# Down blocks of seven products: four sums after the next block's first splits, transfers in another order, two accumulators filled one after the other

## The chip, the cores and the metric

One core of a Trainium2 chip runs the kernel. The metric is the device time of one execution in microseconds; of several runs the median is given. The weights and inputs lie in HBM, and the result is written there.

## The reference, cut to what matters

Two layers work on 512 tokens of width 1024. Each layer mixes (layer 0 by gated projections, layer 1 by attention, both with attention to a memory) and then has a feed-forward part, which is where the change lies:

```python
f = rmsnorm(h, ln_ffn_pre[layer])
f = (jax.nn.silu(f @ w_ffn_gate[layer]) * (f @ w_ffn_up[layer])) @ w_ffn_down[layer]
h = h + rmsnorm(f, ln_ffn_post[layer])
```

The hidden width is 2816, that is 22 blocks of 128. Everything is float32.

## The kernel before, in words

**Exact products by parts.** A float32 operand is split into a high and a low half (`split`, L238 and L239): ScalarE casts the high half (`whi`), VectorE subtracts to get the low one (`wlo`). A product is then three matmuls (`mm3`, L189 to L193): high by high, and two of high by low. TensorE can only begin a product when ScalarE and VectorE have split its weights.

**Seven products for eight.** Two blocks of a matrix product are done by seven products in place of eight, with sums of the operands before and sums of the results after (a scheme of the Strassen kind). There are two sorts of such blocks.

- A gate block and an up block (`Seven`, L1018) work on two blocks of hidden units each. Two loads of 512 KB give four quarters a11, a12, a21, a22. `sums` (L1037) adds them in place (L1041, L1043, L1045, L1046) and splits the first two; `run(n)` does product n. `sevens` (L1088) runs gate, then up, each with the products in the order 1, 7, 2, 6, 4, 3, 5. The results lie in PSUM: tile `a` (called `p` in the code) for products 1, 6 and 5, tile `e` for 7 and 4, tile `x` for 2 and 3. After product 1, ScalarE copies `a` to `s1` (L1059), and product 6 goes on adding to the same `a`. A product is 12 matmuls of 256 columns.
- A down block (`DownSeven`, L1182, and `down_sevens`, L1228) takes four hidden blocks, as two units a and b, to the 1024 outputs of all four token blocks. It has six accumulators of 128x512 in PSUM: two in `chain` (tiles `yc`), two in `shared` (`ys`) and two in `lows` (`yl`), one of each pair for the first and one for the second token block of a half. A product of one unit into one accumulator is three matmuls of 512 columns.

**Where results gather.** `ys[tb][dh]` (tiles `y` in the profile) are eight tiles of 128x512 in SBUF, for four token blocks tb and two output halves dh. A result is added to them in one of two ways. `put` (L1230) has ScalarE copy the accumulator to a tile `yo` (L1232), and GpSimd issue a transfer of 256 KB that adds it to `y` (L1234). Or VectorE adds the accumulator directly (L1262, L1265, L1268). An addition to a tile waits for the one before it on the same tile.

**The order of a down block.** Products 1 (chain), 7 (shared), 2 (lows) of unit a; then of unit b product 1, `put` of the chain to (x, 0), product 7, `put` of shared to (x, 1) and to (x + 2, 1); product 6 of both into the chain, whose value so far ScalarE copies into `shared` (L1256); product 2 of unit b; product 5 of both (chain), `put` to (x + 2, 1), and VectorE adds lows to (x, 0) (L1262); product 4 of both into shared, added to (x, 1) by L1265; product 3 of both into the chain, added to (x + 2, 0) by L1268. Here x is 0 or 1. `both` does a product of unit a into the two accumulators, then that of unit b.

**Groups.** `feed_forward` (L1113) does, per layer, five groups of four hidden blocks: two pairs of gate and up blocks, then a down block. The fifth group has no down block; its result goes through `tail_of`. So there are four down blocks in each layer, eight in all, and each is followed by a gate block. While these run, VectorE makes the splits, the sums of quarters and the sums of results, all in one queue in order; ScalarE casts and copies; SyncE issues the loads of weights (four buffers `raw` of 512 KB, taken in turn); GpSimd issues the adding transfers. Eight buffers each serve `whi` and `wlo`, taken in turn.

**What sets the order.** A framework orders the instructions of each engine from the order of the code and its own guess of times; `tc.high_priority` and `behind` push some forward or back. In the program before, VectorE's queue at a down block's end has the two sums L1265 ahead of the next gate block's second split, and the two sums L1268 ahead of L1046 and of the split of product 7.

Of the kernel before, what the change touches and what calls it, by code (L numbers as in the profile page):

```python
# [11 lines left out]
ALU = mybir.AluOpType  # L12
# [3 lines left out]
P = 128  # L16
# [24 lines left out]
def hybrid(ctx: ExitStack, tc: tile.TileContext, i: dict, out: bass.AP):  # L41
# [17 lines left out]
    def act(s, dt=F32R, shape=(P, T)):  # L59
        return ap.tile(list(shape), dt, tag="a", name=name(s))  # L60

    def plain(s, shape=(P, T), dt=F32):
        return yp.tile(list(shape), dt, tag="y", name=name(s))

    def prob(s, shape=(P, T)):
        return tp.tile(list(shape), F32, tag="p", name=name(s), bufs=6)
# [4 lines left out]
    def small(s, n=4, dt=F32):  # L71
        return sp.tile([P, n], dt, tag=f"s{n}", name=name(s))

    def ps(tag, shape=(P, T), s="ps"):
        return pp.tile(list(shape), F32, tag=tag, name=name(s), bufs=2 if tag == "tr" else 3)

    V, A, PE, G = nc.vector, nc.scalar, nc.tensor, nc.gpsimd
# [102 lines left out]
    def down_weights(layer, k, dh, aside=False):  # L180
        return moving_pair(i["w_down"][layer, 4 * dh : 4 * dh + 4, :, k : k + 2, :]
                           .rearrange("m p k c -> p m (k c)"), aside)
# [6 lines left out]
    def mm3(o, w, x, start, stop, more=False):  # L189

        PE.matmul(o, w[0], x[0], start=start, stop=False, skip_group_check=more)  # L191
        PE.matmul(o, w[0], x[1], start=False, stop=False, skip_group_check=more)  # L192
        return PE.matmul(o, w[1], x[0], start=False, stop=stop, skip_group_check=more)  # L193
# [44 lines left out]
    def split(src, hi, lo, eng=None):  # L238
        last_parts[:] = A.copy(hi, src), (eng or V).tensor_sub(lo, src, hi)  # L239
# [6 lines left out]
    @contextmanager  # L246
    def behind(some):

        with ExitStack() as s:
            for ins in some:  # L250
                s.enter_context(tc.issue_after(ins.ins))
            yield
# [832 lines left out]

    ended = [None]

    def sevens(pair, plain_first, opens=False):  # L1088

        if not plain_first:  # L1090
            for make in pair:
                u = make()
                with behind(ended if opens else ()):
                    u.sums()
                opens = False
                for n in (1, 7, 2, 6, 4, 3, 5):
                    u.run(n)
                u.end()
            return
        us = []  # L1100
        for make in pair:
            us.append(make())
            us[-1].sums()
            for n in (1, 2, 3):
                us[-1].run(n)
        for some in ((7, 6), (4, 5)):
            for u in us:
                for n in some:
                    u.run(n)
        for u in us:  # L1110
            u.end()

    def feed_forward(layer, phase, xp, meanwhile=None):  # L1113
# [24 lines left out]
        def up_rows(row, u, fs, done):  # L1138
            if row:
                V.scalar_tensor_tensor(out=u, in0=u, scalar=-1.0, in1=gates[1], op0=ALU.mult, op1=ALU.mult)  # L1140
            else:
                V.tensor_mul(u, u, gates[0])
            if done:
                done(row, u)
            else:
                split(u, *fs[len(fs) - 2 + row])
# [35 lines left out]
        class DownSeven:  # L1182
# [30 lines left out]
                split_aside(src, *(t.rearrange("p (m c) -> p m c", m=4) for t in pair), aside)  # L1213
                return pair

            def product(self, outs, n, start, stop):
                w = self.w[n]
                if n == 2:
                    w = self.parts(w)
                    V.tensor_add(self.a[1], self.a[0], self.a[1])  # L1220
                    self.w[3] = self.a[1]
                elif n != 1:
                    w = self.parts(w)
                for x, o in enumerate(outs):
                    c = slice(x * P, (x + 1) * P)
                    mm3(o, tuple(t[:, c] for t in self.x[n]), w, start, stop, True)

        def down_sevens(us, pairs):  # L1228

            def put(x, *where):  # L1230
                some = prob("yo")
                A.copy(some, x)  # L1232
                for tb, dh in where:
                    G.dma_start(ys[tb][dh], some, accum_op=ALU.add)  # L1234

            def both(outs, n):
                a.product(outs, n, False, False)
                b.product(outs, n, False, True)

            a, b = us  # L1240
            a.sums(pairs[0])
            chain, shared, lows = ([ps(t, s=n) for _ in range(2)] for t, n in (("tr", "yc"), ("lg", "ys"), ("mm", "yl")))
            a.product(chain, 1, True, False)
            a.product(shared, 7, True, False)
            a.product(lows, 2, True, False)
            b.sums(pairs[1])
            b.product(chain, 1, False, True)
            for x in range(2):
                put(chain[x], (x, 0))
            b.product(shared, 7, False, True)  # L1250
            for x in range(2):
                put(shared[x], (x, 1), (x + 2, 1))
            both(chain, 6)
            with tc.high_priority():
                for x in range(2):
                    A.copy(shared[x], chain[x])  # L1256
            b.product(lows, 2, False, True)
            both(chain, 5)
            for x in range(2):
                put(chain[x], (x + 2, 1))  # L1260
            for x in range(2):
                V.tensor_add(ys[x][0], lows[x], ys[x][0])  # L1262
            both(shared, 4)
            for x in range(2):
                V.tensor_add(ys[x][1], shared[x], ys[x][1])  # L1265
            both(chain, 3)
            for x in range(2):
                V.tensor_add(ys[x + 2][0], chain[x], ys[x + 2][0])  # L1268

        fs = [(act("fhi"), act("flo")) for _ in range(2)]  # L1270

# [8 lines left out]
        a, close = boundary(phase, G_MIX_POST + layer, G_FFN_PRE + layer, nnorm, rb, first, evac_first, scaled)  # L1280
        w = [down_weights(layer, 0, dh) for dh in range(2)]
# [3 lines left out]
        ys = [[plain("y") for _ in range(2)] for _ in range(TB)]  # L1285
        for tb in range(TB):
            for dh in range(2):
                o = ps("lg" if dh else "mm", s="y")
                for k in range(2):
                    token_products(o, fs[k], w[dh][k], tb, k == 0, k == 1)  # L1290
                A.copy(ys[tb][dh], o)

        for gi, (k0, k1) in enumerate(groups):
            fs, pairs, downs = [], [], []
            for m in range(k0, k1, 2):
                if meanwhile and m == k1 - 2 and gi == len(groups) - 1:
                    next(meanwhile)
                if gi < len(groups) - 1:
                    pairs.append(Inner(m < k1 - 2))
                    if m > k0:  # L1300
                        downs.append(DownSeven(m, True))
                else:
                    fs += [(act("fhi"), act("flo")) for _ in range(2)]
                sevens((lambda: Seven(xs, lambda n: i["w_gate"][layer, m + n], "mm", gate_rows),
                        lambda: Seven(xs, lambda n: i["w_up"][layer, m + n], "lg",
                                      lambda row, t: up_rows(row, t, fs, pairs and pairs[-1]))), m == 2, m == k0)
            nk = k1 - k0
            if gi == len(groups) - 1:
                if layer:
                    with behind([gates[2]]):  # L1310
                        A.preload_act_table_set("natural_log_exp_and_others")
                if meanwhile:
                    next(meanwhile)

                eps = small("eps")
                V.tensor_mul(eps, nnorm.r4, nnorm.r4)
                V.reciprocal(eps, eps)
                V.tensor_scalar_mul(eps, eps, RMS_EPS)
                return tail_of(fs, lambda kp, dh, aside, k0=k0: down_weights(layer, k0 + 2 * kp, dh, aside), ys, eps,
                               layer == 1)  # L1320
            down_sevens([DownSeven(k0, False)] + downs, pairs)


    def layer_b(phase, fp):
# [194 lines left out]
    with tc.tile_pool(name="ffn0", bufs=4) as xp:  # L1519
        phase = feed_forward(0, phase, xp, memory())  # L1520
    with tc.tile_pool(name="fox", bufs=1) as fp:
        phase = layer_b(phase, fp)
    with tc.tile_pool(name="ffn1", bufs=4) as xp:
        tail, ys = feed_forward(1, phase, xp)
# [97 lines left out]
```

## Time and profile before

| what | value |
|---|---|
| median of 3 runs | 1107.38 us |
| the three runs | 1107.38, 1107.46, 1104.4 us |
| the profiled execution, its own time | 1104.82 us |
| its span, first to last instruction | 1103.1 us |
| mean granted TensorE clock | 0.998 |
| busy: TensorE, VectorE, ScalarE, GpSimd | 98%, 88%, 68%, 9% |
| mean traffic of the DMA queues | 127 GB/s |

The table gives whole-span figures. Matmuls are pipelined, and the profile draws one of 256 columns 0.28 us long where the next starts sooner, so a busy TensorE shows only its longer waits as idle. In the lines shown below, `out<-in` are tiles by the program's names, `x` with a number is a count, and a bracket at the end of a row gives the idle time of the engine just before it and what ended that. PEld is TensorE's loading of weights, DVE is VectorE, ACT ScalarE, POOL GpSimd, SP SyncE; a q behind an engine is its queue.

### The profile page before, as it was taken

Reading aid. Unit: us, or ns where it says so; the run is one execution under the profiler, and the core shown is the slowest. Engines: PE = TensorE matmul, PEld = TensorE weight load, DVE = VectorE, ACT = ScalarE, POOL = GpSimd, SP = SyncE. Lnnn points to the kernel's source line nnn. Section 1 sums busy time; section 2 is a strip of 40 time slices with the busy share of each in tenths; the row PEclk is TensorE's granted clock in tenths of the full one; section 3 lists DMA queues with packets and bytes.
Section 4 is the critical chain, followed back from the end, with each engine's and each line's share of the span. In section 5 each row is a group of like instructions: output and inputs, shape, how many; then the busy total and the mean of one; then the engine's idle time right before and its main releaser. Section 6 shows DMA issues by size and latency. Waiting matters only on the chain.

```text
span 1103.1 us, 19756 instructions
## 1 busy us (share of the span) xinstructions
PE 1082.6 (98%) x7266; PEld 983.3 (89%) x7267; DVE 970.7 (88%) x1942; ACT 754.5 (68%) x1588; POOL 93.8 (9%) x120
## 2 busy tenths in 40 slices
PE   9999999999999999999999999999999999999998
PEld 7998889997979899998988998889997979899996
DVE  7879759998999999997968789868999989999986
ACT  7776578665756757677746788868666756756664
POOL 0000000002020201101000000000002020201100
PEclk9999999999999999999999999999999999999999
DMA  7521331338464664746222654531338464564722
GB/s 269 160 82 51 120 116 39 115 97 191 120 158 125 136 173 97 207 134 193 68 86 59 154 136 120 148 115 40 115 97 191 116 159 129 116 173 106 180 97 77
DMA packets 83992, 139.64 MB, mean 127 GB/s; under 512 B 6772, under 2 KB 49800, under 8 KB 83896
## 3 DMA queue, kind: packets, MB, share of 16 engines
q1 hardware_dynamic: 71480, 116.57, 34.4%
q0 software_dynamic: 11712, 21.50, 11.7%
q8 instruction: 57, 0.93, 0.4%
q10 hardware_dynamic: 704, 0.32, 0.1%
q14 instruction: 39, 0.32, 0.1%
HBM read 105.23 MB, written 2.10 MB: 97 GB/s over the span
## 4 chain that ended last, share of the span: by engine, by line
PE 85%; DVE 5%; DMA 5%; ACT 3%; issue 1%; SPq 1%; POOL 0%; DVEq 0%; ACTq 0%
PE a L193 5%; PE a L192 5%; PE a L191 5%; PE y L191 4%; PE y L193 4%; PE y L192 4%; PE ps L191 4%; PE ps L193 4%; PE ps L192 4%; DMA y<-yo 4%; PE e L193 3%; PE e L192 3%; PE e L191 3%; PE x L193 3%; PE x L192 3%; PE x L191 3%
## 5 line engine op out<-in xcount | busy, mean ns | idle before, releaser
L239 ACT CAST whi<-raw 128x512 fp32r<-128x512 f32 x444 | 260.7, 619 | 117.9 <-DVE raw L1045 58.2
L239 DVE TENSOR_TENSOR wlo<-raw,whi 128x512 fp32r<-128x512 f32 x444 | 290.6, 682 | 21.0 <-ACT whi L239 20.3
L193 PE MATMUL x<-xshi,wlo 128*128 128x256 f32 x320 | 90.4, 282 | 0.2 <-DVE wlo L239 0.2
L192 PE MATMUL x<-xslo,whi 128*128 128x256 f32 x320 | 90.1, 282 | 0.0
L191 PE MATMUL x<-xshi,whi 128*128 128x256 f32 x320 | 90.1, 282 | 0.0
L192 PE MATMUL a<-xslo,whi 128*128 128x256 f32 x320 | 89.9, 281 | 0.0
L191 PE MATMUL a<-xshi,whi 128*128 128x256 f32 x320 | 89.8, 281 | 0.0
L193 PE MATMUL a<-xshi,wlo 128*128 128x256 f32 x320 | 89.7, 281 | 0.0
L1234 POOL DMA_DIRECT2D y<-yo x64 | 55.5, 1143 | 196.9 <-ACT yo L1232 135.0
L191 PE MATMUL ps<-xshi,whi 128*128 128x256 f32 (+1 forms) x224 | 68.4, 306 | 0.0
L192 PE MATMUL ps<-xslo,whi 128*128 128x256 f32 (+1 forms) x224 | 66.7, 298 | 0.0
L193 PE MATMUL ps<-xshi,wlo 128*128 128x256 f32 (+1 forms) x224 | 66.3, 298 | 0.0
L239 ACT CAST whi<-s 128x512 fp32r<-128x512 f32 x56 | 34.7, 620 | 41.0 <-DVE s L1205 25.0
L193 PEld LDWEIGHTS x<-xshi,wlo 128*128 128x128 f32 x320 | 60.6, 189 | 0.4 <-DVE wlo L239 0.4
L191 PEld LDWEIGHTS a<-xshi,whi 128*128 128x128 f32 x320 | 60.2, 188 | 0.4
L192 PEld LDWEIGHTS a<-xslo,whi 128*128 128x128 f32 x320 | 60.2, 188 | 0.4
L192 PEld LDWEIGHTS x<-xslo,whi 128*128 128x128 f32 x320 | 60.5, 189 | 0.0
L191 PEld LDWEIGHTS x<-xshi,whi 128*128 128x128 f32 x320 | 60.5, 189 | 0.0
L193 PEld LDWEIGHTS a<-xshi,wlo 128*128 128x128 f32 x320 | 60.2, 188 | 0.0
L193 PE MATMUL e<-t3hi,wlo 128*128 128x256 f32 x160 | 45.7, 286 | 10.5 <-DVE wlo L239 10.5
L191 PE MATMUL y<-whi,mixedhi 128*128 128x512 f32 x128 | 51.3, 401 | 0.0
L192 PE MATMUL y<-wlo,mixedhi 128*128 128x512 f32 x128 | 50.6, 395 | 0.0
(352 smaller groups left out, 3637.4 us busy)
## 6 DMA issues: line engine op xcount, KB each, us to landing
raw<-in_w_gate SPq DMA_DIRECT2D x44, 512.0 KB, 3.7
raw<-in_w_up SPq DMA_DIRECT2D x44, 512.0 KB, 5.3
y<-yo POOLq DMA_DIRECT2D x64, 256.0 KB, 5.8
raw<-in_w_down SPq DMA_DIRECT2D x28, 512.0 KB, 4.6
raw<-in_w_out SPq DMA_DIRECT2D x16, 512.0 KB, 4.0
wd<-in_w_down SPq DMA_DIRECT2D x32, 256.0 KB, 8.8
flo<-s POOLq DMA_DIRECT2D x16, 256.0 KB, 5.1
raw<-in_w_b_q SPq DMA_DIRECT2D x8, 512.0 KB, 4.4
```

Source lines behind the costliest of these rows:

```text
L191: PE.matmul(o, w[0], x[0], start=start, stop=False, skip_group_check=more)
L192: PE.matmul(o, w[0], x[1], start=False, stop=False, skip_group_check=more)
L193: return PE.matmul(o, w[1], x[0], start=False, stop=stop, skip_group_check=more)
L239: last_parts[:] = A.copy(hi, src), (eng or V).tensor_sub(lo, src, hi)
L1234: G.dma_start(ys[tb][dh], some, accum_op=ALU.add)
```

## The change

Three edits, all to the down blocks.

1. **Four sums put off.** The last four additions of VectorE, L1265 and L1268, are no longer done at the end of `down_sevens`. It returns them as a function `rest`, with those of the chain now first, and `sevens` calls it in the next group's first gate block, after `run(2)`.
2. **Transfers in another order.** After product 7, the transfers of both accumulators to (x, 1) are issued first, then both to (x + 2, 1). Before, the two transfers of one accumulator stood together. On GpSimd's queue the eight transfers of a block went to (0,0), (1,0), (0,1), (2,1), (1,1), (3,1), (2,1), (3,1); now they go to (0,0), (1,0), (0,1), (1,1), (2,1), (3,1), (2,1), (3,1).
3. **Token block first.** `both` makes the splits of both units first, and then does units a and b into the first accumulator, and units a and b into the second.

```diff
-    def sevens(pair, plain_first, opens=False):
+    def sevens(pair, plain_first, opens=False, rest=None):
...
                 for n in (1, 7, 2, 6, 4, 3, 5):
                     u.run(n)
+                    if rest and n == 2:
+                        rest()
+                        rest = None
                 u.end()
...
+            def product(self, outs, n, start, stop):
+                w = self.weights(n)
                 for x, o in enumerate(outs):
-                    c = slice(x * P, (x + 1) * P)
-                    mm3(o, tuple(t[:, c] for t in self.x[n]), w, start, stop, True)
+                    self.one(o, x, n, w, start, stop)
+
+            def one(self, o, x, n, w, start, stop):
+                c = slice(x * P, (x + 1) * P)
+                mm3(o, tuple(t[:, c] for t in self.x[n]), w, start, stop, True)
...
             def both(outs, n):
-                a.product(outs, n, False, False)
-                b.product(outs, n, False, True)
+                ws = [u.weights(n) for u in us]
+                for x, o in enumerate(outs):
+                    for u, w in zip(us, ws):
+                        u.one(o, x, n, w, False, u is b)
...
             b.product(shared, 7, False, True)
+            both_sums = [put(shared[x], (x, 1)) for x in range(2)]
             for x in range(2):
-                put(shared[x], (x, 1), (x + 2, 1))
+                G.dma_start(ys[x + 2][1], both_sums[x], accum_op=ALU.add)
...
             both(shared, 4)
-            for x in range(2):
-                V.tensor_add(ys[x][1], shared[x], ys[x][1])
             both(chain, 3)
-            for x in range(2):
-                V.tensor_add(ys[x + 2][0], chain[x], ys[x + 2][0])
+
+            def rest():
+                for x in range(2):
+                    V.tensor_add(ys[x + 2][0], chain[x], ys[x + 2][0])
+                for x in range(2):
+                    V.tensor_add(ys[x][1], shared[x], ys[x][1])
+
+            return rest
...
-            down_sevens([DownSeven(k0, False)] + downs, pairs)
+            rest = down_sevens([DownSeven(k0, False)] + downs, pairs)
```

`weights(n)` is the part of the old `product` that splits the weights of product n; `put` now takes one destination and returns its tile `yo`.

In these rows the lines of the changed kernel are its own: its L1281 and L1283 are L1268 and L1265 of the kernel before. VectorE at the end of the first down block, before (`raw_3323` and `raw_3325` are the next gate block's weights, `s_7` its sum for product 7, `ys` and `yc` the accumulators):

```order
L1043 TENSOR_TENSOR raw_3325<-raw_3325 128x512
L1265 TENSOR_TENSOR y_2472<-ys_3149,y_2472 128x512
L1265 TENSOR_TENSOR y_2474<-ys_3150,y_2474 128x512
L239 TENSOR_TENSOR wlo_3340<-raw_3323,whi_3339 128x512
L1045 TENSOR_TENSOR raw_3323<-raw_3325,raw_3323 128x512
L1268 TENSOR_TENSOR y_2475<-yc_3147,y_2475 128x512
L1268 TENSOR_TENSOR y_2477<-yc_3148,y_2477 128x512
L1046 TENSOR_TENSOR raw_3323<-raw_3323 128x512
L239 TENSOR_TENSOR wlo_3359<-s_7_3332,whi_3358 128x512
L239 TENSOR_TENSOR wlo_3388<-raw_3323,whi_3387 128x512
```

The same place of VectorE's queue in the changed kernel, where the gate block's weights are `raw_3319` and `raw_3321`:

```order
L1043 TENSOR_TENSOR raw_3321<-raw_3321 128x512
L239 TENSOR_TENSOR wlo_3336<-raw_3319,whi_3335 128x512
L1045 TENSOR_TENSOR raw_3319<-raw_3321,raw_3319 128x512
L239 TENSOR_TENSOR wlo_3355<-s_7_3328,whi_3354 128x512
L1046 TENSOR_TENSOR raw_3319<-raw_3319 128x512
L1281 TENSOR_TENSOR y_2475<-yc_3147,y_2475 128x512
L1281 TENSOR_TENSOR y_2477<-yc_3148,y_2477 128x512
L1283 TENSOR_TENSOR y_2472<-ys_3149,y_2472 128x512
L1283 TENSOR_TENSOR y_2474<-ys_3150,y_2474 128x512
L239 TENSOR_TENSOR wlo_3388<-raw_3319,whi_3387 128x512
```

The four sums have moved behind the second split, L1045, the split of product 7 and L1046, and stand ahead of the split of product 6 (`wlo_3388`); all eight block ends read like this, and nothing else moves on VectorE.

ScalarE from the gate block's cast for product 7 on, before (`a_3328` is the result of its product 1, `raw_3460` the first load of the up block):

```order
L239 CAST whi_3358<-s_7_3332 128x512
L239 CAST whi_3387<-raw_3323 128x512
L239 CAST whi_3404<-raw_3325 128x512
L1059 COPY s_5_3330<-a_3328 128x256
L239 CAST whi_3420<-raw_3323 128x512
L239 CAST whi_3436<-raw_3325 128x512
L239 CAST whi_3471<-raw_3460 128x512
L239 CAST whi_3476<-raw_3460 128x512
L1074 COPY s_5_3331<-e_3329 128x256
```

The same place of ScalarE's queue in the changed kernel, where the result of product 1 is `a_3324`:

```order
L239 CAST whi_3354<-s_7_3328 128x512
L239 CAST whi_3387<-raw_3319 128x512
L239 CAST whi_3404<-raw_3321 128x512
L239 CAST whi_3420<-raw_3319 128x512
L239 CAST whi_3436<-raw_3321 128x512
L239 CAST whi_3471<-raw_3460 128x512
L239 CAST whi_3476<-raw_3460 128x512
L1059 COPY s_5_3326<-a_3324 128x256
L1074 COPY s_5_3327<-e_3325 128x256
```

The copy of product 1's result has moved behind four casts, two of them of the up block's weights; nothing else moves on ScalarE. On TensorE, products 5, 4 and 3 of the down blocks stand accumulator by accumulator, while the order of product 6, and of everything ahead of it in the block, is unchanged; in the gate block behind it, products 7 and 2 now follow one another, where before the matmuls of product 2 stood between those of product 7. SyncE's order is unchanged.

More of the change, by code (lines that the diff above doesn't have):

```diff
@@ L1214, in parts, with weights @@
                 return pair
-            def product(self, outs, n, start, stop):
+            def weights(self, n):
                 w = self.w[n]
@@ L1223, in product, with put @@
                     w = self.parts(w)
+                return w
+            def product(self, outs, n, start, stop):
+                w = self.weights(n)
                 for x, o in enumerate(outs):
-                    c = slice(x * P, (x + 1) * P)
-                    mm3(o, tuple(t[:, c] for t in self.x[n]), w, start, stop, True)
+                    self.one(o, x, n, w, start, stop)
+            def one(self, o, x, n, w, start, stop):
+                c = slice(x * P, (x + 1) * P)
+                mm3(o, tuple(t[:, c] for t in self.x[n]), w, start, stop, True)
         def down_sevens(us, pairs):
-            def put(x, *where):
+            def put(x, to):
                 some = prob("yo")
                 A.copy(some, x)
-                for tb, dh in where:
-                    G.dma_start(ys[tb][dh], some, accum_op=ALU.add)
+                G.dma_start(ys[to[0]][to[1]], some, accum_op=ALU.add)
+                return some
             def both(outs, n):
-                a.product(outs, n, False, False)
-                b.product(outs, n, False, True)
+                ws = [u.weights(n) for u in us]
+                for x, o in enumerate(outs):
+                    for u, w in zip(us, ws):
+                        u.one(o, x, n, w, False, u is b)
             a, b = us
@@ L1291, in feed_forward @@
                 A.copy(ys[tb][dh], o)
+        rest = None
         for gi, (k0, k1) in enumerate(groups):
@@ L1305, in feed_forward @@
                         lambda: Seven(xs, lambda n: i["w_up"][layer, m + n], "lg",
-                                      lambda row, t: up_rows(row, t, fs, pairs and pairs[-1]))), m == 2, m == k0)
+                                      lambda row, t: up_rows(row, t, fs, pairs and pairs[-1]))), m == 2, m == k0, m == k0 and rest)
             nk = k1 - k0
```

## The prediction

> **What bounds the kernel now.** I read, in this order, the busy shares of the page, who waited for whom on TensorE, the busy time by stretches, and the timeline of one block boundary on VectorE and on TensorE.
>
> The page's span and the first line of its busy part:
>
> ```profile
> span 1103.1 us, 19756 instructions
> ...
> PE 1082.6 (98%) x7266; PEld 983.3 (89%) x7267; DVE 970.7 (88%) x1942; ACT 754.5 (68%) x1588; POOL 93.8 (9%) x120
> ```
>
> TensorE is the bound: 1103.1 - 1082.6 = 20.5 us of the span is not under a matmul. No work is taken away by this change, so all that it can win lies in TensorE's waits. TensorE's waits, longest first (total us, times, longest):
>
> ```profile
> PE e L193 <- DVE wlo L239: 10.5, 6, 2.4
> PE yc L191 <- ACT ys L1256: 2.5, 8, 0.3
> ...
> PE x L193 <- DVE wlo L239: 0.2, 1, 0.2
> ```
>
> There are eight down blocks in the program, four in each layer. Six times TensorE waits in product 7 of a gate block (tile e) for the low half of a weight, which VectorE makes. Eight times it waits within a down block for ScalarE's copy of a running sum. So 13.2 of the 20.5 us belong to the down blocks and to what follows them.
>
> VectorE's own load in a stretch of gate and up products (first row) and around a down block (second row):
>
> ```profile
> 335.00:369.00 34.00, 34.00 (x286) 33.91 (x286) 33.85 (x62) 22.40 (x46) 1.72 (x2) 1.00 0.43 128
> 369.00:397.00 28.00, 26.21 (x139) 21.63 (x138) 25.61 (x46) 17.61 (x35) 6.98 (x8) 1.00 0.75 167
> ```
>
> The third busy figure is VectorE: 33.85 of 34.00 us in the first, 25.61 of 28.00 in the second. Between blocks it has no slack at all; its only idle time, 2.4 us, lies at the block's end. What it idles for there, from the answer on the line of the two sums L1265:
>
> ```profile
>   DMA y<-yo: 9.0, 4
>   PE yc L193: 6.4, 3
>   PE ys L193: 2.0, 7
> ```
>
> That is 17.4 us over the eight blocks. Now VectorE at the second block's end:
>
> ```profile
> 321.32 0.69 DVE L1041 TENSOR_TENSOR s<-raw,raw 128x512 f32<-128x512 f32 x1
> 321.93 0.69 DVE L239 TENSOR_TENSOR wlo<-raw,whi 128x512 fp32r<-128x512 f32 x1
> 322.53 0.69 DVE L1043 TENSOR_TENSOR raw<-raw 128x512 f32<-128x512 f32 x1
> 323.52 0.69 DVE L1265 TENSOR_TENSOR y<-ys,y 128x512 f32<-128x512 f32 x1 [0.30 <-PE ys L193]
> 326.35 0.69 DVE L1265 TENSOR_TENSOR y<-ys,y 128x512 f32<-128x512 f32 x1 [2.14 <-PE yc L193]
> 326.96 0.68 DVE L239 TENSOR_TENSOR wlo<-raw,whi 128x512 fp32r<-128x512 f32 x1
> 327.56 0.68 DVE L1045 TENSOR_TENSOR raw<-raw,raw 128x512 f32<-128x512 f32 x1
> 328.16 1.28 DVE L1268 TENSOR_TENSOR y<-yc,y 128x512 f32<-128x512 f32 x2
> 329.36 0.68 DVE L1046 TENSOR_TENSOR raw<-raw 128x512 f32<-128x512 f32 x1
> 329.96 0.68 DVE L239 TENSOR_TENSOR wlo<-s,whi 128x512 fp32r<-128x512 f32 x1
> 330.56 2.49 DVE L239 TENSOR_TENSOR wlo<-raw,whi 128x512 fp32r<-128x512 f32 x4
> ```
>
> One instruction follows another every 0.60 us, until the second sum L1265, which stands still for 2.14 us. Behind it in VectorE's queue stands all that the next gate block needs. TensorE in the same place:
>
> ```profile
> 326.56 0.40 PE L193 MATMUL yc<-whi,flo 128*128 128x512 f32 x1
> 326.80 0.28 PE L191 MATMUL a<-xshi,whi 128*128 128x256 f32 x1
> ...
> 328.93 0.28 PE L192 MATMUL x<-xslo,whi 128*128 128x256 f32 x1
> 330.69 0.38 PE L193 MATMUL e<-t3hi,wlo 128*128 128x256 f32 x1 [1.49 <-DVE wlo L239]
> 330.91 0.28 PE L191 MATMUL e<-t3hi,whi 128*128 128x256 f32 x1
> ```
>
> It runs through the gate's first product, turns to what it has, and stops at 328.93 until the split that VectorE ended at 329.96 + 0.68 = 330.64. What the second sum waits for is not the matmul that the row names (a wait for several semaphores) but a transfer. The block's fourth and fifth transfer, issued at 317.6 and 318.2:
>
> ```profile
> L1234 POOL DMA_DIRECT2D y<-yo x2: 1197/1364/1530, 317.6 to 318.2; - x2
> ...
> DMA to landing us min/median/max: 6.7/7.4/8.1
> ```
>
> The later one lands at 318.2 + 8.1 = 326.3, and the sum starts at 326.35. It is the accumulating transfer into the second token block, which the sum must follow.
>
> **The change, part by part.**
>
> **Four sums put off.** Followed in the second block with the rows above: the step of 0.60 us continues after L1043 (322.53), so the second split starts at 323.1, L1045 at 323.7, product 7's split at 324.3 (ends 325.0), L1046 at 324.9 (ends 325.6). TensorE needs product 7's split only at 326.80 plus 14 matmuls: the 18 from 326.80 to 328.93 show a step of 0.118, so at 328.5. The wait of product 7 is gone with 3.5 us in hand.
>
> What is late next? The sums now wait for product 3. Token block first, the first accumulator ends six matmuls of 0.23 us before the second: last start 326.56 - 1.39 = 325.17, end 0.40 later, so its sum runs from 325.6. The second ends at 326.96, so VectorE idles some 0.7 us (326.3 to 327.0) with the other three sums and product 6's split queued behind it; then sums at 327.0, 327.6, 328.2 and product 6's split from 328.8 to 329.5. TensorE reaches product 6 after three products of 12 matmuls, 326.80 + 3 x 1.42 = 331.05, and its low half one or two matmuls later, 331.3. Margin 1.8 us. The four sums' 2.4 us of VectorE are hidden by the three gate products that are ready by then; without this cover they would cost up to 2.4 us a block.
>
> So from here both engines run on as they do now, only earlier: TensorE by the wait, VectorE likewise (its first split of the four now ends at 330.56 + 0.68 = 331.24, then at 329.5: 1.8 us earlier). That VectorE can follow matters, since it has no slack for the next 40 us.
>
> The price of a wait is more than its printed idle time. From 328.93 to 330.69 is 1.76 us, 1.64 over the step of 0.118, where 1.49 is printed; and the next step is 0.22. So add 0.15 + 0.10 for each. Waits for wlo: 10.5 + 0.2 + 7 x 0.25 = 12.5 us.
>
> **The clock.** TensorE after the first block's wait, and the granted clock (the seventh figure, PEclk) in two equal stretches behind it:
>
> ```profile
> 267.39 0.39 PE L193 MATMUL e<-t3hi,wlo 128*128 128x256 f32 x1 [2.21 <-DVE wlo L239]
> ```
>
> ```profile
> 268.60:272.00 3.40, 3.40 (x18) 3.40 (x18) 3.40 (x6) 1.30 (x3) 0.00 (x0) 0.51 0.53 148
> 272.20:275.60 3.40, 3.40 (x31) 3.40 (x30) 2.03 (x4) 1.76 (x4) 0.00 (x0) 1.00 0.35 139
> ```
>
> For 3.4 us the clock was half, 18 matmuls where 31 fit: 13 x 0.118 = 1.5 us. It follows a wait of 2.21; I take it as that wait's and count it gone. The longest wait, 2.4, elsewhere, was not followed by one in these rows. The Trainium skill (TensorE: Matmul & The Clock Gate, What's actually happening) has the clock fall after at least one idle window of about 3.4 us, and that window free-running. By that rule a wait of 2.2 us could not bring it, the 1.5 us would have another cause and stay, and the sum would be 12.5; the trace, with a fall 1.2 us after a wait of 2.21, speaks against it.
>
> **Transfers in order of need.** The one into the second token block goes out fourth instead of fifth, and the fourth place lands, by the row above, at 317.6 + 6.7 = 324.3, 2 us earlier. Gain now: nothing, since its sum has moved to 328.2 and the present landing at 326.3 is already in time. The two transfers of product 5 wait behind it on GpSimd's queue for the two that moved back; only the next block's transfers stand behind those. The longest landing of any of these transfers:
>
> ```profile
> DMA to landing us min/median/max: 3.3/5.8/11.3
> ```
>
> Even 11.3 after 318.2 is 329.5, 1.3 late for the sum and inside product 6's 1.8.
>
> **Token block first.** The second unit's split is needed three matmuls (0.70 us) earlier. Its nearest case, product 5 of the second block: the split, and the matmul at whose place the second unit now begins:
>
> ```profile
> 317.12 0.68 DVE L239 TENSOR_TENSOR wlo<-wd,whi 128x512 fp32r<-128x512 f32 x1
> ```
>
> ```profile
> 319.14 0.40 PE L191 MATMUL yc<-whi,fhi 128*128 128x512 f32 x1
> ```
>
> Ready at 317.80, wanted at 319.37 at the soonest: 1.6 us in hand, cost nothing. Nor does it win the eight waits for ScalarE's copy: the order of product 6 is the same, and product 5's first matmul still enters the accumulator that is being copied. 2.5 + 8 x 0.25 = 4.5 us stay.
>
> **ScalarE's copy L1059.** It moves behind four more casts, and product 6 must wait for it, because it saves the sum that product 6 adds to. Now:
>
> ```profile
> 328.27 1.14 ACT L239 CAST whi<-raw 128x512 fp32r<-128x512 f32 x2 [5.61 <-DVE raw L1045]
> 329.32 0.36 ACT L1059 COPY s<-a 128x256 f32<-128x256 f32 x1
> ```
>
> The casts can then start at 324.4 with L1045. The last two take the up block's weights, and the last of all a buffer that the gate's first product must leave (328.2), so it ends near 329.0 and the copy near 329.4: earlier than now (329.68), 1.6 before product 6. Cost nothing, if the up weights have landed; issue and landing:
>
> ```profile
> 319.67 1.51 SPq L144 DMA_DIRECT2D raw<-in_w_up  x2
> ```
>
> ```profile
> DMA to landing us min/median/max: 3.5/5.3/6.6
> ```
>
> At 6.6 they are there at 326.3. They would be felt from 331.05 - 0.36 - 1.16 = 329.5 on, 9.9 us after issue.
>
> **Sum.** 12.5 + 1.5 = 14.0 us against the profiled execution: 1104.8 - 14.0 = 1090.8. That execution lies near the lowest of the three runs (1104.4), while the other two are 2.6 to 3.0 above. Two more stretches at half clock (2 x 1.5, an estimate, shown by no row) would explain them; they would go with the waits. So I forecast the median too at 1090.8 and leave 2.6 for the upper end.
>
> **The rivals.**
>
> *VectorE is the bound* (chance 0.10). For it: 33.85 of 34.00. Then the win is the idle time that VectorE loses: 17.4, less some 0.7 at each of eight blocks (the wait for product 3's second sum), 11.8. 1104.8 - 11.8 = 1093.0. Against it: its shift of 1.8 us in the second block equals TensorE's 1.64 + 0.10.
>
> *The clock falls anyway* (0.07): 1104.8 - 12.5 = 1092.3.
>
> *The wait only moves* (0.04): TensorE passes product 7 and stops at product 6 for the split behind the sums. That needs a sum that starts after 328.2 + 1.8 = 330.0, a landing of 11.8 us or more. At 13.4 us each block loses 1.6 again, 12.8 in all: 1104.8 - 14.0 + 12.8 = 1103.6, no change by what this kernel's measurement can tell (0.3%, 3.3 us). Against it: 11.3 is the longest recorded.
>
> *Slower, by the up weights* (0.04): ScalarE's copy stands behind casts that wait for a load. Every us beyond 9.9 after issue costs each block one. At 12.5 it is 8 x 2.6 = 20.8: 1104.8 - 14.0 + 20.8 = 1111.6. It turns to slower than now from 9.9 + 14.0 / 8 = 11.7. Against it: 6.6 at most.
>
> **How the numbers follow.** Forecast 0.75, the four rivals 0.10, 0.07, 0.04, 0.04. The range takes 1090.8, 1092.3 and 1093.0 with 2.6 on top for the spread of the runs: up to 1095.6, say 1096.0. Downwards, half of the 4.5 us of ScalarE's copies might go with them, if ScalarE comes to them earlier: 1088.5. The two rivals outside hold 0.08. Faster is 0.75 + 0.10 + 0.07 = 0.92, same 0.04, slower 0.04.
>
> **What would show it.** Right: no row "PE e <- DVE wlo" above 0.3 us, the eight waits for the copy still near 2.5 us, VectorE idle some 0.7 us at each block's second sum of product 3 and nowhere else at the block's end, and the clock at 1.00 after each block. Wrong: a wait of "PE a" for wlo or of product 6 for ScalarE's copy; new idle time of TensorE in the down blocks at the second unit's splits; or waits gone and the time not, which would mean that VectorE sets the pace.

## The result, and the profile after

The changed kernel takes 1091.05 us (median of 4 runs, 1090.35 to 1093.4), the kernel before in runs beside it 1107.42 (4 runs, 1104.4 to 1107.73): a ratio of 0.9862, interval 0.9839 to 0.9885. The forecast was 1090.8. One run of the changed kernel, 1093.4, lies 1.9 us above the highest of the other three; its mean clock is listed as 0.998, theirs as 0.999. The profiled execution of the changed kernel took 1091.55 us, 13.3 less than that of the kernel before (1104.82); its clock was at 1.00 all through, but for the first 6.6 us and the last 3.2 of its record. Lines of the changed kernel are its own: L1281 are the sums of the chain's accumulators, L1283 those of the shared ones.

The page's span and the first line of its busy part:

```profile
span 1089.8 us, 19773 instructions
...
PE 1079.4 (99%) x7267; PEld 981.4 (90%) x7267; DVE 970.6 (89%) x1942; ACT 756.1 (69%) x1588; POOL 93.8 (9%) x120
```

What is left of TensorE's waits (total us, times, longest):

```profile
PE yc L191 <- ACT ys L1269: 2.5, 8, 0.3
PE ys L191 <- DVE s L1080: 1.4, 2, 0.8
```

The row "PE e <- DVE wlo" (10.5 us) and its neighbour "PE x" (0.2) are gone. The eight waits for ScalarE's copy stand where they were, at the same 2.5. One row is new beside the first profile of the kernel before: 1.4 us for a tile s of VectorE.

The busy figures make the ledger. Time not under a matmul was 20.5 us and is 1089.8 - 1079.4 = 10.4, so 10.1 less: 10.7 of waits for wlo gone, 1.4 new, 0.6 less for a tile alo at the program's start, the rest small. Time under a matmul fell by 1082.6 - 1079.4 = 3.2, although the matmuls are the same: the stretch at half clock (1.5) and the slow restarts behind seven waits (7 x 0.25 = 1.75) add up to that. Together 13.3.

VectorE at the second block's end, in the changed kernel (start, length, engine, line; in brackets its idle time and who ended it):

```profile
320.81 0.68 DVE L239 TENSOR_TENSOR wlo<-s,whi 128x512 fp32r<-128x512 f32 x1
321.41 0.68 DVE L1046 TENSOR_TENSOR raw<-raw 128x512 f32<-128x512 f32 x1
322.04 0.69 DVE L1281 TENSOR_TENSOR y<-yc,y 128x512 f32<-128x512 f32 x1
323.43 0.69 DVE L1281 TENSOR_TENSOR y<-yc,y 128x512 f32<-128x512 f32 x1 [0.70 <-PE yc L193]
324.04 1.28 DVE L1283 TENSOR_TENSOR y<-ys,y 128x512 f32<-128x512 f32 x2
325.23 2.49 DVE L239 TENSOR_TENSOR wlo<-raw,whi 128x512 fp32r<-128x512 f32 x4
```

TensorE in the same place (first matmul of the gate's product 1, first low half of product 7, and product 6):

```profile
323.23 0.28 PE L191 MATMUL a<-xshi,whi 128*128 128x256 f32 x1
...
324.89 0.28 PE L193 MATMUL e<-t3hi,wlo 128*128 128x256 f32 x1
...
327.42 0.28 PE L191 MATMUL a<-d2hi,whi 128*128 128x256 f32 x1
...
327.66 0.28 PE L193 MATMUL a<-d2hi,wlo 128*128 128x256 f32 x1
```

Product 7's split ends at 320.81 + 0.68 = 321.49, and TensorE takes it at 324.89: 3.4 us in hand (3.5 were forecast). Then VectorE stands 0.70 us at the second sum of product 3 (forecast "some 0.7"). Product 6's split starts at 325.23 and, one step of 0.60 with 0.08 of its tail, is ready at 325.9; TensorE takes it at 327.66, 1.75 later (1.8 forecast).

Over all blocks, what VectorE idled for at L1281; the row of L1283 has none:

```profile
  PE yc L193: 4.9, 7
```

ScalarE's copy of product 1's result, behind its last cast:

```profile
324.79 0.62 ACT L239 CAST whi<-raw 128x512 fp32r<-128x512 f32 x1 [0.70 <-PE a L192]
325.32 0.36 ACT L1059 COPY s<-a 128x256 f32<-128x256 f32 x1
```

It ends at 325.68, and product 6, which starts at 327.42, finds it done 1.74 us earlier (1.6 forecast). The cast ahead of it waited for the gate's first product to leave a buffer, as the prediction had it, and not for the up weights.

Last, VectorE between the blocks and around one (third busy figure):

```profile
335.00:369.00 34.00, 34.00 (x264) 32.65 (x263) 33.89 (x64) 22.28 (x47) 1.72 (x2) 1.00 0.38 109
366.00:394.00 28.00, 27.68 (x164) 23.81 (x163) 27.30 (x49) 20.30 (x39) 6.98 (x8) 1.00 0.80 188
```

Around a block VectorE now works 27.30 of 28.00 us, where it worked 25.61.

### The profile page after: what moved, and what is told of

It is laid out like the page before. It is cut to its first block, busy times and chain, and to the rows that moved or that the text cites. A ratio compares the mean times of both kernels' runs of the same rounds, so it can differ in the third digit from the quotient of the medians.

```text
span 1089.8 us, 19773 instructions
## 1 busy us (share of the span) xinstructions
PE 1079.4 (99%) x7267; PEld 981.4 (90%) x7267; DVE 970.6 (89%) x1942; ACT 756.1 (69%) x1588; POOL 93.8 (9%) x120
## 4 chain that ended last, share of the span: by engine, by line
PE 88%; DVE 6%; ACT 3%; issue 1%; DMA 1%; SPq 0%; DVEq 0%; ACTq 0%
PE y L191 5%; PE y L192 5%; PE y L193 5%; PE a L193 4%; PE a L192 4%; PE a L191 4%; PE ps L191 4%; PE ps L193 4%; PE ps L192 4%; PE e L191 3%; PE e L192 3%; PE e L193 3%; PE x L192 3%; PE x L193 3%; PE x L191 3%; PE yc L191 3%
## 5 line engine op out<-in xcount | busy, mean ns | idle before, releaser
L1243 POOL DMA_DIRECT2D y<-yo x48 | 41.4, 954 | 198.1 <-ACT yo L1242 133.1
L193 PE MATMUL y<-whi,mixedlo 128*128 128x512 f32 x128 | 50.4, 394 | 0.0
```

The source lines that it names most:

```text
L1243: G.dma_start(ys[to[0]][to[1]], some, accum_op=ALU.add)
```

## The experiments

Theory: the waits of product 7 came from the second sum L1265, which stood still in VectorE's queue for the landing of its transfer, with the gate's splits behind it. Rivals: TensorE gained by the order of its own matmuls (token block first), or VectorE sets the pace and any idle time that it loses is the gain. The first three experiments keep one of the three edits each, and their code cuts show what is taken back from the changed kernel; the others alter one thing, or two, in the changed kernel. Ratios are against the kernel before in runs on the same chip: 13 runs, median 1106.66 us, for the first three and for ScalarE's copies put first; 7 runs, median 1105.67 us, for the rest.

### The sums put off, alone

Transfers and matmuls in the order of the kernel before:

```
-                ws = [u.weights(n) for u in us]
-                for x, o in enumerate(outs):
-                    for u, w in zip(us, ws):
-                        u.one(o, x, n, w, False, u is b)
+                a.product(outs, n, False, False)
+                b.product(outs, n, False, True)
...
-            both_sums = [put(shared[x], (x, 1)) for x in range(2)]
             for x in range(2):
-                G.dma_start(ys[x + 2][1], both_sums[x], accum_op=ALU.add)
+                some = put(shared[x], (x, 1))
+                G.dma_start(ys[x + 2][1], some, accum_op=ALU.add)
```

> Only the four sums are put off; transfers and products stand as before. Theory of the landing (TensorE waited because the splits stood in VectorE's queue behind a sum that waited for a transfer; it suffices to move the splits ahead): all of the gain, 1091 us, within 1.5 of the whole change, no wait of TensorE for product 7, although the transfer to the second token block still lands fifth. Rival (the three edits are needed together): some of the 14 us stays, 1095 to 1100.

Measured: 1090.24 us (1089.95 to 1090.97), ratio 0.9848, interval 0.9823 to 0.9873. TensorE's longest wait, with no row for wlo among the rest:

```profile
PE yc L191 <- ACT ys L1267: 2.5, 8, 0.3
```

The whole gain comes with this one edit. The 0.8 us by which it lies below the changed kernel are inside both intervals.

### The transfers in order of need, alone

The sums where they stood, matmuls as before:

```
             both(shared, 4)
+            for x in range(2):
+                V.tensor_add(ys[x][1], shared[x], ys[x][1])
             both(chain, 3)
-            def rest():
-                ...
-            return rest
+            for x in range(2):
+                V.tensor_add(ys[x + 2][0], chain[x], ys[x + 2][0])
```

(and the body of `both` as in the experiment above)

> Only the transfers are reordered; the four sums stand where they stood. Theory of the landing: in the second block the fourth transfer landed at 324.3 where the fifth landed at 326.3, so the second sum starts at 324.35; the split of product 7 then ends near 328.9 and TensorE wants it at 329.05. So nearly all of the gain comes from this edit too, 1091 to 1094 us. Rival (the sums' own 2.4 us ahead of the splits cost the time, wherever the transfer lands): waits of 1.2 to 1.6 us stay, 1103 to 1107.

Measured: 1091.12 us (1091.01 to 1091.95), ratio 0.9857, interval 0.9832 to 0.9881. So this edit too brings the whole gain by itself. VectorE at the second block's end, with the two sums in their old place (here L1276):

```profile
318.91 0.69 DVE L1276 TENSOR_TENSOR y<-ys,y 128x512 f32<-128x512 f32 x1 [0.26 <-PE ys L193]
320.25 0.69 DVE L1276 TENSOR_TENSOR y<-ys,y 128x512 f32<-128x512 f32 x1 [0.65 <-DMA y<-yo]
...
323.86 0.68 DVE L239 TENSOR_TENSOR wlo<-s,whi 128x512 fp32r<-128x512 f32 x1
```

The first four transfers of this block, with the time from issue to landing:

```profile
L1243 POOL DMA_DIRECT2D y<-yo x4: 851/1018/1197, 308.1 to 313.0; - x4
...
DMA to landing us min/median/max: 3.3/4.2/7.1
```

The fourth, issued at 313.0, lands at 313.0 + 7.1 = 320.1, and the sum that must follow it starts at 320.25. It still waits for a landing, now 0.65 us where it was 2.14, and this time the row names the DMA. This shows the cause that the prediction had read from two times that agree (326.3 and 326.35). What the shorter wait leaves is hardly anything:

```profile
324.32 0.28 PE L192 MATMUL x<-xslo,whi 128*128 128x256 f32 x1
324.60 0.38 PE L193 MATMUL e<-t3hi,wlo 128*128 128x256 f32 x1
```

Product 7's split ends at 324.54 and TensorE takes it at 324.60, 0.16 us later than a step of 0.12 would have it. In the changed kernel the same split had 3.4 us in hand. The two edits are two cures for one wait, either enough; they do not add.

### Token block first, alone

```
-            both_sums = [put(shared[x], (x, 1)) for x in range(2)]
             for x in range(2):
-                G.dma_start(ys[x + 2][1], both_sums[x], accum_op=ALU.add)
+                some = put(shared[x], (x, 1))
+                G.dma_start(ys[x + 2][1], some, accum_op=ALU.add)
```

(and the sums as in the second experiment)

> Only the products are done accumulator by accumulator. Theory of the landing: the second sum still waits for the fifth transfer, six waits of product 7 stay, 1104 to 1107.5 us. Rival (the earlier end of the first accumulator, or the copies within the block, give part of the gain): 1100 or less.

Measured: 1107.87 us (10 runs, 1104.58 to 1109.41), ratio 0.9999, interval 0.998 to 1.0018. TensorE's waits:

```profile
PE e L193 <- DVE wlo L239: 11.2, 6, 2.4
```

And what VectorE idled for ahead of the two sums (here L1278):

```profile
  DMA y<-yo: 17.5, 7
```

Nothing that can be measured is won or lost, as forecast, though the median lies 0.4 us above the range expected. In the kernel before, this idle time was 9.0 us under the transfer's name and 6.4 under that of product 3's matmuls, 15.4 in all; here 17.5, all under the transfer's. That fits the reading that the DMA had come last there too and that a row for several semaphores can name another; with the edit the matmuls that it named have moved.

### The changed kernel once more

> The changed kernel once more, on the chip of the next three, as their measure: 1090.3 to 1091.5 us.

Measured: 1090.73 us (1090.32 to 1091.51), ratio 0.9856, interval 0.9832 to 0.9879. The new row of TensorE for the tile s, 1.4 us in the first profile, is 0.3 here (once). The difference starts 25 us earlier. VectorE in the first profile:

```profile
219.32 0.69 DVE L1041 TENSOR_TENSOR s<-raw,raw 128x512 f32<-128x512 f32 x1 [0.64 <-DMA raw<-in_w_up]
```

and TensorE, 25 us later:

```profile
244.85 0.50 PE L191 MATMUL ys<-whi,fhi 128*128 128x512 f32 x1 [0.76 <-DVE s L1080]
```

In the repeat the same L1041 started at 219.07 without a wait, 0.25 earlier, and no wait of 0.76 followed. There TensorE's matmul started at 244.61, 0.24 earlier than in the first profile. So the late load had put VectorE back by 0.25 us, which it had not made up 25 us later, and TensorE with it; for the rest of the 0.76, TensorE had only come to this place sooner. A printed wait is not what the wait costs. This is read from two profiles, not tried by itself. The same row stands at the same place, with 0.65 us, in a second profile of the kernel before, so it is not a mark of the change.

### VectorE's idle time at the sums taken away: the shared sums first

Is VectorE the bound now? The two shared sums, ready earlier, go ahead of the chain's, which was meant to take away the 0.70 us that VectorE idles at each block:

```
             def rest():
-                for x in range(2):
-                    V.tensor_add(ys[x + 2][0], chain[x], ys[x + 2][0])
                 for x in range(2):
                     V.tensor_add(ys[x][1], shared[x], ys[x][1])
+                for x in range(2):
+                    V.tensor_add(ys[x + 2][0], chain[x], ys[x + 2][0])
```

> The changed kernel with the two sums of the shared accumulators ahead of those of the chain. Their accumulators are done and their transfers landed by then, so VectorE no longer idles 0.7 us at each of some seven blocks: 4.9 us of its idle time go. Theory (TensorE is the bound again, VectorE follows with time in hand): the time stays within 0.5 us of the changed kernel. Rival (VectorE is the bound): up to 4.9 us less, 1086 us.

Measured: 1090.69 us (1089.83 to 1091.67), ratio 0.9855, interval 0.9831 to 0.9878; 0.04 us below the repeat. The profile's rows of the line that now holds the shared sums have nothing under "sat idle":

```profile
L1281 DVE TENSOR_TENSOR y<-ys,y x16: 685/694/699, 262.2 to 1017.6; 128x512 f32<-128x512 f32 x16
its engine sat idle before it (us, times) until:
who waited for it (us, times):
```

Nor have those of the chain's sums. But the 4.9 us of idle time aren't gone, they have moved. VectorE has a row here that the changed kernel lacks, and in the second block it stands some 7 us later, at the sum that takes up the gate's product 4 (tile e). VectorE's row, the instruction, and TensorE's last matmul of that product:

```profile
DVE s L1079 <- ACT whi L239: 4.8, 7, 0.7
```

```profile
330.75 0.43 DVE L1079 TENSOR_TENSOR s<-e,s 128x256 f32<-128x256 f32 x1 [0.65 <-ACT whi L239]
```

```profile
330.36 0.28 PE L193 MATMUL e<-t,wlo 128*128 128x256 f32 x1
```

That matmul ends at 330.64, just ahead of the sum, so by the times the sum waits for it and not for the cast that the row names. VectorE ran its splits 0.65 us earlier and then stood still for TensorE. So the experiment took no idle time away, and that the time stayed is no proof by itself; what speaks against VectorE setting the pace is that, put ahead, it has to wait for TensorE at the next result, seven times.

### VectorE loaded by 1.2 us more in each block

How far is it from that? Two more instructions of VectorE, of 0.60 us each by the step of its queue, behind the four sums. They leave their tile's values as they are:

```
             def rest():
                 ...
+                for _ in range(2):
+                    V.scalar_tensor_tensor(out=rbc, in0=rbc, scalar=0.0, in1=rbc, op0=ALU.mult, op1=ALU.add)
```

> The changed kernel with two more instructions of VectorE in each block's put-off sums (rbc = 0 x rbc + rbc, 128x512, 0.6 us each); the values stay the same. Theory (VectorE and TensorE are level: VectorE has some 0.7 us a group in hand): 1.2 - 0.7 + what idles still, so 0.5 to 1.1 us for each of some seven groups, 1094 to 1098 us, and TensorE waits for low halves in the down blocks, not in the gate block. Rival (VectorE has room): no change, 1090.5 to 1091.5. Rival (the four sums have no cover left in the gate block): 1.2 us and the restart for each block at product 6, 1101 or more.

Measured: 1098.36 us (1097.09 to 1099.05), ratio 0.9924, interval 0.9895 to 0.9953: 0.4 above the range expected and 7.6 us above the repeat, of 16 x 0.60 = 9.6 added, so 0.95 of 1.2 in each block. TensorE's rows:

```profile
PE x L193 <- DVE wlo L239: 1.4, 1, 1.4
...
PE yl L191 <- ACT whi L239: 1.2, 4, 0.3
PE yc L191 <- ACT yo L1242: 1.2, 6, 0.2
PE ys L191 <- ACT fhi L239: 1.1, 2, 0.5
```

The loss does not come out where the instructions stand, and only once as a wait for a low half, in a gate or up block (tile x), where the expectation had such waits in the down blocks: most rows are short waits in the down blocks for ScalarE's casts and copies. Nor do the printed waits hold all of it: between the profiles of the repeat and of this kernel the time not under a matmul grew by 2.6 us and that under matmuls by 4.2. And the order of the matmuls in those blocks has changed with the extra instructions. How much of the 7.6 is VectorE's load and how much that order isn't separated. What is shown is that two more instructions a block are mostly paid; that they are paid because VectorE follows TensorE closely is a reading.

### ScalarE's two copies ahead of the cast

The waits that stayed, 2.5 us printed, are for two copies L1269 that stand behind a cast in ScalarE's queue. ScalarE around the second block's wait, in the changed kernel, and TensorE's wait:

```profile
313.60 0.63 ACT L239 CAST whi<-raw 128x512 fp32r<-128x512 f32 x1
314.12 1.08 ACT L1269 COPY ys<-yc 128x512 f32<-128x512 f32 x2
```

```profile
314.77 0.50 PE L191 MATMUL yc<-whi,fhi 128*128 128x512 f32 x1 [0.33 <-ACT ys L1269]
```

Product 4's cast, that at 313.60, is put behind the copies:

```
-                for x in range(2):
-                    A.copy(shared[x], chain[x])
+                copies = [A.copy(shared[x], chain[x]) for x in range(2)]
...
-            both(shared, 4)
+            with behind(copies):
+                both(shared, 4)
```

> The changed kernel with ScalarE's two copies of the chain put ahead of the cast of product 3's weights (product 4's splits are ordered behind the copies). The first copy now starts 0.37 us after the matmul that it waits for, because a cast of 0.62 is under way. Theory (the eight waits of 0.3, 0.58 us each with the slower restart, are ScalarE's order): each loses some 0.35 us, 8 x 0.35 = 2.8, 1088 us. Rival (VectorE sets the pace of the whole group, so TensorE meets it later): 1090.5 to 1091.5, and a wait for a low half in its place.

Measured: 1089.03 us (1088.91 to 1089.12), ratio 0.9836, interval 0.9812 to 0.986; 1.7 us below the repeat of the changed kernel (1090.73), whose runs lie all above it. The fastest version here, but only some 60% of the 2.8 us expected. TensorE's waits:

```profile
PE yc L191 <- ACT yo L1242: 1.6, 6, 0.3
...
PE e L193 <- DVE wlo L239: 1.2, 1, 1.2
```

The row for L1269 is gone, and two others have come: six waits for the copies L1242 that feed the transfers, since the order of TensorE's matmuls moved too and product 6 now begins earlier, behind the other two copies of the block; and one wait of 1.2 in product 7 of a later block of gate or up products.

Both alterations of the order together, the shared sums and the copies first:

> Both: the shared sums first and ScalarE's copies ahead of the cast. Theory: as the copies alone, 1088.5 to 1089.3 us. Rival (with the copies first VectorE had become the bound, so its idle time counts now): 1087.5 or less.

Measured: 1089.26 us (1089.0 to 1089.46), ratio 0.9841, interval 0.9818 to 0.9864. The shared sums add nothing here either.

### The clock: two profiles more

One term of the sum, 1.5 us, was put down to a stretch at half clock behind a wait of 2.21. The kernel with token block first alone has two such stretches in its profile, and the points at which its clock changed (269.52 and 395.81) lie 126.29 us apart, 37.0 times the 3.413 that each stretch lasted. Cut into windows of that length, counted from such a point (first busy figure TensorE's, the seventh the granted clock):

```profile
266.10:269.52 3.41, 1.51 (x13) 1.34 (x12) 3.41 (x7) 3.16 (x7) 0.86 (x1) 1.00 1.09 220
269.52:272.93 3.41, 3.41 (x19) 3.41 (x18) 3.41 (x7) 1.22 (x3) 0.00 (x0) 0.50 0.55 163
392.40:395.81 3.41, 1.03 (x9) 0.82 (x8) 3.41 (x7) 2.56 (x6) 0.87 (x1) 1.00 0.61 111
395.81:399.22 3.41, 3.41 (x18) 3.41 (x18) 3.41 (x7) 1.92 (x4) 0.00 (x0) 0.50 0.61 133
```

Two kernels were profiled once more, the kernel before

> The kernel before once more, unchanged, for its clock rows. The granted clock so far changed only at points that lie a multiple of 3.413 us apart, and the stretch at half clock followed a window of that grid in which TensorE was idle 2.12 us; windows with 1.53 us or less were not followed by one. Theory: the idle time within one window of this free-running grid decides, with the bound between 1.53 and 1.90 us (half a window is 1.71). Then every stretch at half clock in this profile starts where such a window with over 1.53 us idle ends, each such stretch is 3.41 us long, and no window with less than 1.53 us is followed by one; time 1104 to 1110, by 0, 1, 2 or 3 stretches of 1.5 us each. Rival: the length of the single wait decides (2.2 us or more), wherever it lies on the grid: then the wait of about 2.4 us in the second layer is followed by a stretch in some profile although it is split over two windows. Other rival: the stretches have nothing to do with the waits: then one starts behind a window without idle time.

and token block first alone

> The kernel with token block first alone once more, for a further set of windows. The theory and the rivals of the repeat of the kernel before: every stretch at half clock starts at the end of a grid window (3.413 us) in which TensorE was idle for over 1.53 us, and none follows a window with less; time 1104 to 1110, 1.5 us for each stretch beyond the least.

They took 1108.41 and 1109.34 us. The kernel before, in two pairs of neighbouring windows around waits:

```profile
265.96:269.37 3.41, 1.71 (x15) 1.50 (x13) 3.41 (x7) 1.68 (x4) 0.86 (x1) 1.00 1.11 281
269.37:272.79 3.42, 3.07 (x26) 3.07 (x27) 3.42 (x7) 2.23 (x6) 0.00 (x0) 1.00 0.67 98
...
911.08:914.49 3.41, 1.03 (x8) 0.82 (x8) 3.41 (x7) 2.64 (x6) 0.86 (x1) 1.00 0.51 93
914.49:917.90 3.41, 3.41 (x19) 3.41 (x18) 3.41 (x6) 1.95 (x4) 0.00 (x0) 0.50 0.60 132
```

Behind the first pair's wait the clock stayed: it took 1.70 us of the one window and 0.35 of the next. The window of the second pair holds a wait of 2.38 us whole, and half clock follows. In the first profile of the same kernel a wait as long lay across a border of the windows:

```profile
906.97:910.38 3.41, 2.07 (x16) 1.67 (x14) 3.09 (x6) 1.16 (x3) 0.00 (x0) 1.00 1.13 290
910.38:913.79 3.41, 2.16 (x18) 2.16 (x19) 3.41 (x6) 2.72 (x6) 0.86 (x1) 1.00 0.51 88
913.79:917.20 3.41, 3.41 (x31) 3.41 (x31) 3.41 (x7) 1.17 (x3) 0.00 (x0) 1.00 0.82 258
```

and no half clock followed. So the length of the wait alone does not decide; how much of one window it takes fits all these cases. Token block first, in its repeat, has two windows more of which TensorE was busy for 0.62 and 0.95, each followed by half clock. With all four profiles cut in this way from 14 us on, every stretch at half clock (six, the program's last microseconds aside) came behind a window that was busy for 1.51 us or less, each such window was followed by one, and no window busy for 1.71 or more was. Half of 3.41 would be a bound that fits; that it is this is not shown.

A seventh stretch does not fit. It lies at the start of the repeat of the kernel before, within the first 14 us:

```profile
6.54:9.96 3.42, 2.23 (x13) 1.62 (x13) 1.75 (x3) 1.92 (x4) 0.00 (x0) 1.00 1.03 353
9.96:13.37 3.41, 3.41 (x16) 3.31 (x16) 3.11 (x6) 2.71 (x5) 0.00 (x0) 0.50 1.02 402
```

Here TensorE was busy for 2.23 of the window, and half clock followed. So the expectation for this profile, that no window idle for less than 1.53 us would be followed by half clock, failed at one of its two stretches. Why the start differs is open.

## Why the prediction was right

**What the second sum waited for, and who stood behind it.** Shown: with the transfer one place earlier on its queue, fourth instead of fifth, and nothing else altered, the waits of product 7 are gone, and where the sum still waits, the row names the DMA at the time of its landing. Reading the row "PE yc" against the landing rather than by its name was the step on which all rested.

**The sums put off.** Right in size and in place: every margin that was worked out ahead (3.5, 0.7, 1.8) is in the trace of after within 0.1 us.

**The wait's price, with its restart.** It fits: 0.25 us for each of seven waits is, with the clock's 1.5, the 3.2 us by which time under matmuls fell. The two were not measured apart.

**The clock.** The term was right, and so was laying it to the wait; more is now known of when it comes. The prediction noted that a wait of 2.4 elsewhere was not followed by half clock. The grid of windows fits that: TensorE was idle for 1.34 us of one window and 1.25 of the next, each less than in any window that half clock followed, but for the one at the program's start. It also bears on the gap between profile and median: the executions of the kernel before list a mean clock from 0.999 (1104.24 us) to 0.994 (1113.52), and 0.005 of 1113 us is 5.6 of these 9.3. By the phase of the grid the same waits cost none, one or more stretches. That fits medians 16.4 apart (1107.42 - 1091.05) beside profiles 13.3 apart; how many stretches the runs without a profile had isn't recorded. The forecast of the median rested on two more stretches that no row showed; the three later profiles with the old waits have two each, though one of these six is the one at the program's start. The Trainium skill (TensorE: Matmul & The Clock Gate, What's actually happening) has a window of 3413 ns that is free-running, and the traces agree: 3.413 us, 37.0 of them between two changes. It has the clock fall after at least one idle window of about 3.4 us; here windows in which TensorE was busy for up to 1.51 us, and one of 2.23, were followed by it, so the measurement decides against reading this as a window with no work in it. The rival that the clock falls anyway fails on the clock's rows: behind the blocks of the changed kernel it stays at 1.00. By its time, 1092.3, it could not be told apart.

**Transfers in order of need: "gain now: nothing".** Right only beside the first edit, as the prediction costed it. By itself the edit is worth 15.5 us (1106.66 - 1091.12), which the prediction did not see: it had the landing of the fourth place 2 us earlier among its numbers, and the wait that would shrink by it (2.14), but went on from the sums' new place.

**Token block first.** Right: no change that can be measured.

**What was missed.** Waits of 1.4 us for the tile s in the first profile, 0.3 in the repeat. With 0.6 less for alo on the other side they come to the 0.75 us between the profiled execution (1091.55) and the forecast. They differ from one execution to the next, with the old order too (0.9 in the second profile of the kernel before); that late loads cause them was followed at one of them only.

**The rivals.** VectorE as the bound would have given 1093.0, which the times alone do not exclude (the ratio's interval, on 1107.42, is 1089.6 to 1094.7). Against it stands that VectorE, put 0.65 us ahead, waited for TensorE; that 9.6 us more of its work cost 7.6 suggests that it is near. The wait didn't move to product 6, which kept 1.75 us, and ScalarE's copy was done 1.74 ahead of it; that copy's point of decision, a landing 11.7 us after issue, was not tried.

## What to carry to other kernels

In a queue that runs in order, an instruction that waits for a slow transfer charges its wait to all behind it: look for it where an engine without slack stands still, check the named releaser against the landings, and move either the instruction behind what is urgent or the transfer ahead in its own queue; one of the two is enough. A wait of TensorE of some 2 us can cost 1.5 more in clock, by where it falls, so a kernel free of such waits can be steadier too (4 runs of the sums alone lie within 1.02 us, 13 of the kernel before beside them within 9.3; but the changed kernel's first 4 runs, with the one of 1093.4, spread by 3.05). When an edit is to take idle time from an engine, look where that engine idles afterwards: here all of it came back 7 us later.

## What the runs showed of the hardware

In four profiles the granted clock of TensorE changed only at the borders of windows of 3.413 us that run on regardless of the program's waits. From 14 us on, behind a window busy for 1.51 us or less it was half for one window, and behind one busy for 1.71 or more it stayed; in the first 14 us of one of them half clock followed a window busy for 2.23. Six accumulating transfers of 256 KB of one block, on GpSimd's queue, land one after the other: the first 3.3 us after issue, the fourth 6.6 to 7.1, the fifth 8.1 to 8.4, the sixth 10.0 to 10.2, so the fourth place instead of the fifth was worth about 2 us of landing (324.3 instead of 326.3 in the kernel before) though issues are only 0.6 apart.
